# Mixer part of a hybrid decoder block: operands of the convolution half one block ahead, the output projection with that half first, loads and splits issued from inside the rows

## The chip, the cores and the metric

The kernel runs on one core of a Trainium2 chip. The metric is device microseconds (us) of one execution. The core has a matrix engine (PE, with its weight loads PEld), three elementwise engines (DVE, ACT, POOL) and a queue engine (SP) that issues DMA transfers; each engine takes its instructions strictly from its own list.

## The reference

One layer on a sequence of 2048 positions with 1024 channels, all in 32-bit floats:

```python
hn = rms_norm(x, g_pre_mix)
proj = hn @ w_in
y_ssm = s5_group_mixer(u_ssm, ...)      # ends in y * sigmoid(y @ w_glu)
y_conv = short_conv_mixer(h_conv, b_gate, c_gate, conv_w)
y = concatenate([rms_norm(y_ssm, g_ssm_out), rms_norm(y_conv, g_conv_out)], axis=-1)
x = x + rms_norm(y @ w_out, g_post_mix)
hn = rms_norm(x, g_pre_mlp)
m = square(relu(hn @ w_up)) @ w_down
x = x + rms_norm(m, g_post_mlp)
```

The change touches the lines from `sigmoid(y @ w_glu)` to `hn @ w_up`.

## The kernel before, in words

Every 32-bit product is made of three matmuls: each operand is split into a high and a low part (`split`, L167 to L169: ACT copies the high part, another engine subtracts it to get the low part), and `mm3` (L86 to L89) adds high by high, high by low and low by high.

The kernel runs in this order: input projections with the state-space part and the short convolution (results go to the DRAM tensors `y_d` and `yc_d`); then the mixer, which is what the change is about; then up (`product`, a scheme with seven products for eight) and down. The mixer works in four blocks of 512 positions:

- `yprep(blk)` (L688) loads four tiles of `y_d` and splits them; `glu(blk)` (L810) multiplies them by the gate weights, four groups of twelve matmuls in PSUM "B" (three buffers), takes the sigmoid on ACT, multiplies on DVE, scales and splits to `mh[blk]`, and adds up squares on POOL (`sumsq`, L788).
- `cprep(blk)` (L799) loads four tiles of `yc_d`, scales and splits them to `mc[blk]`, and adds up squares on DVE.
- `load_wo` (L834) loads and splits the sixteen 128x512 pieces of the output weights; `glu` takes two of its steps after each of its groups.
- `norms(blk, br)` (L847) sums the squares over the partitions with four small matmuls in PSUM "C" (one buffer), and DVE and POOL make the factor `rr` of it.
- `wout(blk)` (L868) makes four rows of 128 positions. A row is four groups of twelve matmuls in PSUM "A" (four buffers): two column halves with `mh` (br 0), then two with `mc` (br 1). ACT copies the first two to the row buffer `o` with the factor (L888), DVE adds the others (L892). Then comes a chain over the whole row: square on ACT, factor on POOL (`rstd`, L121, L122), DVE L898, square, factor, DVE L904; `x1_d` and `hn_d` are stored by SP (L899, L906).
- `hsum(0, t)` (L917) reads `hn_d` back (1 MB), makes five sums on DVE (L924) and stores them to `hs_d`; `xload` and `xbuild` (L929, L938) load a 1 MB operand of up and transpose it on PE; `wprep` (L1007) makes the weights of up.

The buffers that matter: `s2k` (nine of 2 KB a partition), `r4` (four rows, for `x`, for `o`, and for the raw `y` of odd blocks), `c8` (four) and `b8` (fourteen) of 8 KB. PE and POOL run the instructions in the order in which the code issues them; the lists of DVE, ACT and SP are put in order when the program is built. The blocks stand in this order: `cprep(0)`, `yprep(1)`, `glu(0)`, `glu(1)`, `yprep(2)`, `wout(0)`, `glu(2)`, `cprep(1)`, `yprep(3)`, `wout(1)`, `glu(3)`, `cprep(2)`, four `hsum`, `wout(2)`, `cprep(3)`, two `xload`, `wout(3)` with two `xbuild` in it, and then up with the first `wload`, two more `xload` and seven `wprep`.

## Time and profile before

| | us |
|---|---|
| median of 3 runs | 2021.76 |
| the runs | 2017.68 to 2022.14 |
| the profiled execution, its own time | 2021.03 |
| its span, first to last instruction | 2018.8 |
| PE busy in it | 1927.5 (95%) |
| DVE busy in it | 1423.1 (70%) |

The span is the time between the first and the last instruction; the profiled execution took 2.2 us more than its span. The busy time of PE is a modelled one: matmuls overlap, and each is shown with 0.39 us where a new one starts every 0.23 us. What PE lost is therefore read from its idle stretches, from what ended them, and from the granted clock.

### The profile page before, as it was taken

Reading aid. Unit: us, or ns where it says so; the run is one execution under the profiler, and the core shown is the slowest. Engines: PE = TensorE matmul, PEld = TensorE weight load, DVE = VectorE, ACT = ScalarE, POOL = GpSimd, SP = SyncE. Lnnn points to the kernel's source line nnn. Section 1 sums busy time; section 2 is a strip of 40 time slices with the busy share of each in tenths; the row PEclk is TensorE's granted clock in tenths of the full one; section 3 lists DMA queues with packets and bytes.
Section 4 is the critical chain, followed back from the end, with each engine's and each line's share of the span. In section 5 each row is a group of like instructions: output and inputs, shape, how many; then the busy total and the mean of one; then the engine's idle time right before and its main releaser. Section 6 shows DMA issues by size and latency. Waiting matters only on the chain.

```text
span 2018.8 us, 25420 instructions
## 1 busy us (share of the span) xinstructions
PE 1927.5 (95%) x8576; PEld 1573.8 (78%) x8576; DVE 1423.1 (70%) x2046; ACT 839.3 (42%) x1463; POOL 701.0 (35%) x704
## 2 busy tenths in 40 slices
PE   8789999997977989999999999999999999999997
PEld 6667877785755768888888888887888888888886
DVE  8748889858666669888878887876844444539564
ACT  6322232235433335555556555554433343235331
POOL 3295666404333223434432443441522102203220
PEclk9889999999988999999999999999999999999999
DMA  6432243125436655755447343426955545548634
GB/s 199 128 90 82 75 138 124 59 82 159 141 104 210 238 204 191 261 186 204 164 146 261 144 170 141 147 110 231 381 197 187 193 146 177 179 134 282 230 104 146
DMA packets 202002, 340.34 MB, mean 169 GB/s; under 512 B 56336, under 2 KB 64784, under 8 KB 199568
## 3 DMA queue, kind: packets, MB, share of 16 engines
q1 hardware_dynamic: 201728, 338.72, 49.4%
q8 instruction: 67, 1.10, 0.2%
q14 instruction: 63, 0.52, 0.1%
q10 hardware_dynamic: 144, 0.00, 0.0%
HBM read 230.51 MB, written 106.95 MB: 167 GB/s over the span
## 4 chain that ended last, share of the span: by engine, by line
PE 78%; DVE 6%; DMA 5%; issue 4%; POOL 4%; ACT 3%; SPq 0%; DVEq 0%; POOLq 0%; ACTq 0%
PE A L87 16%; PE A L89 16%; PE A L88 16%; PE mm L87 4%; PE B L87 4%; PE B L89 4%; PE B L88 4%; PE mm L88 4%; PE mm L89 4%; DMA raw<-in_xt_dram 2%; DMA s2k<-yc_d 1%; PE C L87 1%; PE C L89 1%; PE C L88 1%; PE B L947 1%
## 5 line engine op out<-in xcount | busy, mean ns | idle before, releaser
L1013 POOL TENSOR_TENSOR t<-b 128x512 f32<-128x512 f32 x155 | 247.0, 1616 | 364.0 <-DVE t L1047 109.3
L87 PE MATMUL A<-b,w 128*128 128x512 f32 x640 | 249.8, 390 | 0.0
L89 PE MATMUL A<-b,w 128*128 128x512 f32 x640 | 249.1, 389 | 0.0
L88 PE MATMUL A<-b,w 128*128 128x512 f32 x640 | 249.0, 389 | 0.0
L1093 POOL TENSOR_TENSOR t<-t,t 128x512 f32<-128x512 f32 x80 | 118.8, 1491 | 362.5 <-DMA t<-in_w_down_dram 358.1
L87 PE MATMUL mm<-xh,wh 128*128 128x512 f32 x496 | 200.4, 404 | 7.3 <-ACT wh L168 7.3
L88 PE MATMUL mm<-xl,wh 128*128 128x512 f32 x496 | 196.5, 396 | 2.6 <-DVE xl L152 2.6
L89 PE MATMUL mm<-xh,wl 128*128 128x512 f32 x496 | 196.0, 395 | 0.2 <-POOL wl L169 0.2
L169 DVE TENSOR_TENSOR b<-w,b 128x512 fp32r<-128x512 f32 x112 | 92.8, 869 | 131.3 <-ACT b L168 131.3
L87 PE MATMUL A<-b,c 128*128 128x512 f32 x448 | 175.1, 391 | 1.5 <-ACT b L168 1.5
L88 PE MATMUL A<-b,c 128*128 128x512 f32 x448 | 175.1, 391 | 0.6 <-DVE b L169 0.6
L89 PE MATMUL A<-b,c 128*128 128x512 f32 x448 | 174.8, 390 | 0.0
L1066 DVE TENSOR_TENSOR t<-t,t 128x512 f32<-128x512 f32 x160 | 127.8, 864 | 36.8 <-ACT t L1020 36.8
L169 DVE TENSOR_TENSOR w<-t,w 128x512 fp32r<-128x512 f32 x160 | 127.8, 814 | 35.8 <-ACT w L168 34.5
L169 DVE TENSOR_TENSOR c<-w,c 128x512 fp32r<-128x512 f32 x112 | 83.3, 782 | 96.1 <-ACT c L168 96.0
L89 PEld LDWEIGHTS A<-b,w 128*128 128x128 f32 x640 | 120.1, 188 | 25.0
L87 PEld LDWEIGHTS A<-b,w 128*128 128x128 f32 x640 | 120.1, 188 | 24.8
L88 PEld LDWEIGHTS A<-b,w 128*128 128x128 f32 x640 | 120.2, 188 | 24.5
L168 ACT ACTIVATE b<-w 128x512 fp32r<-128x512 f32 x112 | 64.6, 622 | 159.4 <-PE C L89 146.3
L87 PE MATMUL B<-b,b 128*128 128x512 f32 x336 | 130.7, 389 | 0.0
L88 PE MATMUL B<-b,b 128*128 128x512 f32 x336 | 130.7, 389 | 0.0
L89 PE MATMUL B<-b,b 128*128 128x512 f32 x336 | 130.7, 389 | 0.0
(421 smaller groups left out, 4439.5 us busy)
## 6 DMA issues: line engine op xcount, KB each, us to landing
hid_d<-t SPq DMA_DIRECT2D x224, 256.0 KB
w<-hid_d SPq DMA_DIRECT2D x224, 256.0 KB
t<-in_w_down_dram SPq DMA_DIRECT2D x192, 256.0 KB
b<-in_w_up_dram SPq DMA_DIRECT2D x64, 512.0 KB
raw<-in_xt_dram SPq DMA_DIRECT2D x48, 256.0 KB
raw<-in_w_cv_dram SPq DMA_DIRECT2D x48, 256.0 KB
b<-hs_d SPq DMA_DIRECT2D x10, 1024.0 KB
r<-in_x_dram SPq DMA_DIRECT2D x16, 512.0 KB
```

The costliest lines, as they stand in the source:

```text
L87: T.matmul(ps, lh, rh, start=start, stop=False)
L88: T.matmul(ps, lh, rl, start=False, stop=False)
L89: T.matmul(ps, ll, rh, start=False, stop=stop)
L168: A.activation(dst_h, raw, AF.Copy)
L169: eng.tensor_tensor(dst_l, raw, dst_h.bitcast(F32), op=ALU.subtract)
L947: T.transpose(pt[:, t * P:(t + 1) * P], r[:, t, k * P:(k + 1) * P], ident)
L1013: eng.tensor_tensor(src, q[0], q[1], op=pm_op[LEFT[j][1]])
L1066: V.tensor_tensor(src, q[0], q[1], op=pm_op[LEFT[j][1]])
L1093: G.tensor_tensor(r[0], r[0], r[1], op=pm_op[RIGHT[j][1]])
```

## The change

What was issued between the blocks is issued inside them. `yprep`, `cprep` and `hsum` become generators that first issue all their loads; `wout` takes a step of such a generator after each of its sixteen groups. `cprep(blk + 1)` runs within `wout(blk)`, and a row takes the `mc` half (br 1) first. The conv half of the output weights is loaded and split first, with the low parts on DVE as before; the low parts of the other half are made on POOL. The squares for the norms are made in place. `r4` is now two pools of two, `xx` and `o`. A new pool of eight 2 KB tiles (`w2a`) lives through mixer and up in place of `h2` and of half of the pool `w2` of up (the other half is `w2b`). `c8` now also holds `mc` of odd blocks. The first `wload`, three `xload`, four `wprep` and the two `xbuild` stand in `wout(3)`.

```diff
@@ def yprep @@
-        if blk % 2 == 1:
+        if blk == 1:
             a, b = c8(), c8()
...
+            rs = [t[:, 512 * j:512 * j + 512] for t in (r4("o"), r4("o")) for j in range(2)]
         else:
-            hl = [(h2(), h2()) for q in range(4)]
...
+            hl = [(w2a(), w2a()) for q in range(4)]
             rs = [s2k() for _ in range(4)]
...
+        yhl[blk] = hl
+        yield
+        for q in range(4):
...
             A.activation(nat(h), r, AF.Copy)
             V.tensor_tensor(nat(l), r, nat(h.bitcast(F32)), op=ALU.subtract)
+            yield
@@ def sumsq, def cprep @@
-    def sumsq(blk, br, i, src):
-        t = s2k()
+    def sumsq(blk, br, i, t):
         if br:
-            A.activation(t, src, AF.Square)
+            A.activation(t, t, AF.Square)
         else:
-            G.tensor_tensor(t, src, src, op=ALU.mult)
+            G.tensor_tensor(t, t, t, op=ALU.mult)
...
-        h, l = b8(), b8()
+        h, l = (c8(), c8()) if blk % 2 else (b8(), b8())
...
+        for i in range(-2, 4):
+            if i < 2:
+                raw[i + 2] = s2k()
+                nc.sync.dma_start(out=raw[i + 2], in_=yc_d[i + 2][:, blk * BLK:(blk + 1) * BLK])
+                if i < 0:
+                    continue
+            if i == 0:
+                yield
+            yc = raw[i]
@@ def glu, def load_wo @@
-            if blk and m == (3 if blk == 1 else 1):
-                norms(blk - 1, 0)
...
-        for h in range(2):
+        for h in (1, 0):
...
-                           w_out[k * P:(k + 1) * P, dh * 512:dh * 512 + 512], V)
+                           w_out[k * P:(k + 1) * P, dh * 512:dh * 512 + 512], V if h else G)
@@ def wout @@
-            for br, m in ((0, mh[blk]), (1, mc[blk])):
+            for br, m in ((1, mc[blk]), (0, mh[blk])):
...
-                    if t == 0 and dh == 0 and br == 1:
-                        norms(blk, 1)
-                        if blk == 2:
-                            norms(3, 0)
+                    if t == 0 and dh == 0:
+                        norms(blk, br)
                     rr = rrs[blk, br]
-                    if br == 0:
+                    if br:
                         A.activation(o[:, sl], ps, AF.Copy, scale=rr[:, t:t + 1])
...
+                    next(aside, None)
+            if t == 3:
+                run(aside)
@@ the order of the blocks @@
+    def first():
+        wload(0)
+        for j in ORDER[:2]:
+            xload(0, j)
+        yield
+        for i, j in enumerate(ORDER[:2]):
+            for n in ORDER[2 * i:2 * i + 2]:
+                yield
+                wprep(0, n, V, s2k)
+            yield from xbuild(0, j)
+        xload(0, ORDER[2])
+
+    wout(0, chain(yprep(2), cprep(1)))
+    glu(2)
+    wout(1, chain(yprep(3), cprep(2)))
+    glu(3)
+    wout(2, chain(cprep(3), *(hsum(0, t, lambda: c8(F32)) for t in range(4))))
+    wout(3, first())
@@ def wprep, def dload @@
-        h, l = w2(), w2()
+        h, l = (w2a(), w2a()) if j in ORDER[:4] else (w2b(), w2b())
...
-                raws = [[w2(F32)] for _ in range(2)]
+                raws = [[(w2b if side else w2a)(F32)] for _ in range(2)]
```

In the built programs SP issues 1225 transfers before and after, DVE has eight instructions fewer and POOL eight more. Three places show what moved.

The first is POOL at the end of `glu(1)`. These are its rows before (L793 and L797 are the squares and sums of the `glu` blocks, L860 is the factor of the first norms):

```order
L793 TENSOR_TENSOR s2k<-s2k 128x512 x2
L797 TENSOR_TENSOR s2k<-s2k 128x512
L793 TENSOR_TENSOR s2k<-s2k 128x512
L797 TENSOR_TENSOR s2k<-s2k 128x512
L793 TENSOR_TENSOR s2k<-s2k 128x512
L797 TENSOR_TENSOR s2k<-s2k 128x512
L860 TENSOR_TENSOR rr_4959<-sr,nhalf 128x4
```

And these are the rows there of the changed kernel, where the same three operations stand on L798, L802 and L871, and L170 is the low part of a piece of the output weights:

```order
L170 TENSOR_TENSOR b_4859<-s2k,b_4859 128x512
L170 TENSOR_TENSOR b_4860<-s2k,b_4860 128x512
L798 TENSOR_TENSOR s2k<-s2k 128x512
L802 TENSOR_TENSOR s2k<-s2k 128x512
L170 TENSOR_TENSOR b_4857<-s2k,b_4857 128x512
L170 TENSOR_TENSOR b_4858<-s2k,b_4858 128x512
L798 TENSOR_TENSOR s2k<-s2k 128x512
L802 TENSOR_TENSOR s2k<-s2k 128x512
L170 TENSOR_TENSOR b_4859<-s2k,b_4859 128x512
L170 TENSOR_TENSOR b_4860<-s2k,b_4860 128x512
L871 TENSOR_TENSOR rr_4974<-sr,nhalf 128x4
```

Two low parts stand behind each square of `glu(1)`, and the factor of the first norms stands behind the last of them.

The second place is SP, where the conv operands of block 1 are loaded. Before, the loads stand behind the stores of the last row of `wout(0)` (`x_d_93` and `hn_d_109`):

```order
L700 DMA r_5433<-y_d_85 128x8x64
L899 DMA x_d_93<-r_5232 128x1024
L906 DMA hn_d_109<-r_5234 256x1x512
L872 DMA r_5446<-in_x_dram 128x1024
L804 DMA s2k<-yc_d_86 128x512
L804 DMA s2k<-yc_d_87 128x512
L804 DMA s2k<-yc_d_88 128x512
L804 DMA s2k<-yc_d_89 128x512
```

In the changed kernel they stand ahead of the stores of the first row of `wout(0)`:

```order
L704 DMA s2k<-y_d_84 128x8x64
L704 DMA s2k<-y_d_85 128x8x64
L811 DMA s2k<-yc_d_86 128x512
L811 DMA s2k<-yc_d_87 128x512
L811 DMA s2k<-yc_d_88 128x512
L811 DMA s2k<-yc_d_89 128x512
L910 DMA x_d_90<-xx 128x1024
L917 DMA hn_d_106<-o 256x1x512
```

The loads moved from the end of the block to its first row, some three rows of `wout` earlier.

The third place is SP at the end of `wout(2)`. Before, the two operands of up (`b_6283`, `b_6285`, from `hs_d`) are loaded ahead of the stores of the block's last row (`x_d_101`, `hn_d_113`):

```order
L899 DMA x_d_100<-r_6104 128x1024
L906 DMA hn_d_112<-r_6106 256x1x512
L872 DMA r_6287<-in_x_dram 128x1024
L932 DMA b_6283<-hs_d_114 128x2048
L932 DMA b_6285<-hs_d_116 128x2048
L899 DMA x_d_101<-r_6179 128x1024
L906 DMA hn_d_113<-r_6181 256x1x512
```

In the changed kernel the stores of the last `hsum` (L937), those stores and the weights of up come first:

```order
L910 DMA x_d_100<-xx 128x1024
L917 DMA hn_d_112<-o 256x1x512
L937 DMA hs_d_114<-c_6108 128x512
L937 DMA hs_d_115<-c_6108 128x512
L937 DMA hs_d_116<-c_6108 128x512
L937 DMA hs_d_117<-c_6108 128x512
L937 DMA hs_d_118<-c_6107 128x512
L884 DMA xx<-in_x_dram 128x1024
L910 DMA x_d_101<-xx 128x1024
L917 DMA hn_d_113<-o 256x1x512
L986 DMA b_6282<-in_w_up_dram 128x1024 x2
L944 DMA b_6285<-hs_d_114 128x2048
```

The load of the first operand (`b_6285`) moved behind the stores of the last row; its first transposes on PE moved by one group only, from ahead of the last group of the first row of `wout(3)` to behind it.

## Rows read from the trace of the kernel before

**Rows 1.** Stages: window, its length, busy PE, PEld, DVE, ACT, POOL (instructions), clock, DMA share, GB/s.
```profile
455.80:511.50 55.70, 42.97 (x162) 31.48 (x162) 45.02 (x51) 29.63 (x47) 23.38 (x16) 0.88 0.56 164
511.50:556.10 44.60, 44.60 (x202) 36.98 (x201) 29.99 (x32) 20.93 (x31) 13.80 (x17) 1.00 0.39 130
556.10:616.70 60.60, 48.82 (x201) 38.04 (x200) 36.38 (x39) 18.36 (x31) 20.27 (x21) 0.92 0.30 102
616.70:628.50 11.80, 11.80 (x57) 9.88 (x56) 7.57 (x9) 5.26 (x9) 4.37 (x5) 1.00 0.28 100
628.50:694.70 66.20, 54.20 (x209) 42.20 (x209) 46.71 (x61) 23.65 (x40) 19.98 (x22) 0.82 0.75 254
694.70:747.10 52.40, 50.06 (x233) 41.33 (x231) 32.75 (x41) 18.86 (x33) 10.98 (x17) 0.97 0.58 206
747.10:763.00 15.90, 5.73 (x14) 3.93 (x14) 13.58 (x15) 6.23 (x11) 7.62 (x7) 0.61 0.91 327
770.00:1370.00 600.00, 600.00 (x2732) 499.10 (x2731) 498.20 (x675) 333.62 (x592) 238.53 (x150) 1.00 0.48 173
```

**Rows 2.** Waits of PE from 455 to 765: us in total, times, longest.
```profile
PE A L87 <- ACT b L805: 16.1, 4, 8.2
PE A L87 <- ACT w L168: 9.2, 1, 9.2
PE B L87 <- ACT s2k L819: 6.7, 4, 1.9
PE A L89 <- DVE b L806: 3.9, 4, 2.0
PE A L88 <- DVE b L169: 3.7, 4, 1.9
PE A L87 <- ACT r L888: 3.4, 2, 2.0
```

**Rows 3.** Timeline of PE around the second half of the first row of `wout(1)`.
```profile
558.53 0.39 PE L89 MATMUL A<-b,b 128*128 128x512 f32 x1
...
561.25 0.39 PE L89 MATMUL A<-b,b 128*128 128x512 f32 x1
569.80 0.79 PE L87 MATMUL A<-b,b 128*128 128x512 f32 x1 [8.17 <-ACT b L805]
...
572.24 0.63 PE L88 MATMUL A<-b,b 128*128 128x512 f32 x1
```

**Rows 4.** Groups of POOL from 455.8 to 511.5: busy us, mean ns, idle before.
```profile
L793 POOL TENSOR_TENSOR s2k<-s2k 128x512 f32<-128x512 f32 x8 | 10.9, 1367 | 32.2 <-DVE s2k L820 32.2
L797 POOL TENSOR_TENSOR s2k<-s2k 128x512 f32<-128x512 f32 x6 | 9.6, 1605 | 0.5
L860 POOL TENSOR_TENSOR rr<-sr,nhalf 128x4 f32<-128x4 f32 x2 | 2.9, 1428 | 2.7 <-DVE sr L857 2.7
```

**Rows 5.** Low parts (L169) on POOL and DVE: ns min/median/max, first and last start.
```profile
L169 DVE TENSOR_TENSOR b<-s2k,b x16: 676/686/1780, 475.6 to 509.0; 128x512 fp32r<-128x512 f32 x16
...
L169 POOL TENSOR_TENSOR wl<-raw,wh x4: 1322/1626/1831, 7.3 to 20.7; 128x512 fp32r<-128x512 f32 x4
```

**Rows 6.** Timeline of DVE: the chain of the last row of `wout(3)`.
```profile
746.75 0.75 DVE L892 SCALAR_TENSOR_TENSOR r<-A,rr,r 128x512 f32<-128x512 f32 x1 [1.44 <-PE A L89]
...
754.24 0.75 DVE L904 TENSOR_SCALAR r<-r,s 128x1024 f32<-128x1024 f32 x1 [0.92 <-POOL s L122]
```

**Rows 7.** Sums of `hsum` on DVE, 628 to 706: busy us, mean ns, idle.
```profile
L924 DVE TENSOR_TENSOR c<-c 128x512 f32<-128x512 f32 x20 | 13.5, 735 | 0.0
```

**Rows 8.** The critical chain: start, us; the load of an operand of up.
```profile
695.86 5.95 DMA b<-hs_d
```

**Rows 9.** Waits of the queue SP, 555 to 765: total us, times, longest.
```profile
SPq L920 <- DMA hs_d<-c: 3.3, 2, 3.2
```

**Rows 10.** DMA issues by line: count and KB of each.
```profile
hs_d<-c SPq DMA_DIRECT2D x20, 256.0 KB
...
c<-hn_d SPq DMA_DIRECT2D x4, 1024.0 KB
```

More of the change, by code (lines that the diff above doesn't have):

```diff
@@ L2 @@
 from contextlib import ExitStack
+from itertools import chain
 import concourse.bass as bass
@@ L656, in open_left @@
         pool("xl", "XL")
+        pool("sbw", "W")
         mid("sbl", "L")
@@ L667, in b8, with w2a, r4 @@
         return sb["XR"].tile([P, 4, 512], dt, name="b8", bufs=14)
-    def h2(dt=F32R):
-        return sb["L"].tile([P, 512], dt, name="h2", bufs=8)
+    def w2a(dt=F32R):
+        return sb["W"].tile([P, 512], dt, name="w2a", bufs=8)
     def s2k():
         return sb["L"].tile([P, 512], F32, name="s2k", bufs=9)
-    def r4():
-        return sb["R"].tile([P, D], F32, name="r4", bufs=4)
+    def r4(name):
+        return sb["R"].tile([P, D], F32, name=name, bufs=2)
     def small(name, n, bufs=2):
@@ L742, in block_kernel @@
                 open_left()
-                yprep(0)
+                run(yprep(0))
                 gluh, glul = c8(), c8()
@@ L799, in cprep @@
     def cprep(blk):
-        h, l = b8(), b8()
+        h, l = (c8(), c8()) if blk % 2 else (b8(), b8())
         mc[blk] = (h, l)
-        for i in range(4):
-            yc = s2k()
-            nc.sync.dma_start(out=yc, in_=yc_d[i][:, blk * BLK:(blk + 1) * BLK])
+        raw = {}
+        for i in range(-2, 4):
[7 more added lines that the diff above has]
+            yc = raw[i]
             A.activation(h[:, i, :], yc, AF.Copy, scale=gcv[:, i:i + 1])
@@ L826, in glu @@
             sumsq(blk, 0, m, sg)
[L827 to L828 removed]
             for _ in range(2):
                 next(wo_steps, None)
[L832 removed]
+    wo = {}
     def load_wo():
[L835 removed]
+        for h in (1, 0):
             for k in range(4 * h, 4 * h + 4):
[L837 removed]
+                wo[k] = b8()
             for dh in range(2):
@@ L866, in junk, with wout @@
         return sb["R"].tile([P, D], BF16, name="junk", bufs=1)
-    def wout(blk):
+    def wout(blk, aside=()):
+        aside = iter(aside)
         for t in range(4):
             tt = 4 * blk + t
-            xx = r4()
+            xx = r4("xx")
             nc.sync.dma_start(out=xx, in_=x[tt * P:(tt + 1) * P, :])
-            o = r4()
-            for br, m in ((0, mh[blk]), (1, mc[blk])):
+            o = r4("o")
+            for br, m in ((1, mc[blk]), (0, mh[blk])):
                 for dh in range(2):
@@ L940, in xbuild @@
         r = rows.pop((hf, j))
-        get = c8 if j in ORDER[:2] else b8
+        get = c8 if j in ORDER[:4:2] else b8
         h, l = get(), get()
@@ L950, in xbuild @@
             yield
-    steps = iter(())
-    def step(n=1):
-        for _ in range(n):
-            next(steps, None)
-    cprep(0)
+    run(yprep(1))
+    cprep0 = cprep(0)
+    next(cprep0)
     gss = sb["XR"].tile([P, 24], F32, name="gss", bufs=1)[:, :4]
     nc.sync.dma_start(out=gss, in_=g_ssm)
-    yprep(1)
+    run(cprep0)
     gpo = sb["R"].tile([P, D], F32, name="gp", bufs=1)
@@ L968, in block_kernel @@
     glu(1)
-    for _ in wo_steps:
-        pass
-    yprep(2)
-    wout(0)
-    glu(2)
-    cprep(1)
-    yprep(3)
-    wout(1)
-    glu(3)
-    cprep(2)
-    for t in range(4):
-        hsum(0, t, lambda: c8(F32))
-    wout(2)
-    cprep(3)
-    for j in ORDER[:2]:
-        xload(0, j)
-    steps = (None for j in ORDER[:2] for _ in xbuild(0, j))
-    wout(3)
-    pm_.close()
-    mid("sbu", "U")
-    def w2(dt=F32R):
-        return sb["U"].tile([P, 512], dt, name="w2", bufs=16)
-    def t2(shape=(P, 512), dt=F32):
-        return sb["U"].tile(list(shape), dt, name="t2", bufs=14)
+    run(wo_steps)
     NF = DFF // 256
@@ L1005, in wload, with wprep @@
             nc.sync.dma_start(out=r[:, 2 * i:2 * i + 2, :], in_=w_up[2 * f + i])
-    def wprep(n, j, eng=G):
+    def wprep(n, j, eng=G, tmp=None):
         r = wraw[n]
@@ L1011, in wprep, with w2b, t2 @@
         if len(q) > 1:
-            src = t2()
+            src = (tmp or t2)()
             eng.tensor_tensor(src, q[0], q[1], op=pm_op[LEFT[j][1]])
-        h, l = w2(), w2()
+        h, l = (w2a(), w2a()) if j in ORDER[:4] else (w2b(), w2b())
         split(h, l, src, V)
         W[n, j] = h, l
+    def first():
+        wload(0)
+        for j in ORDER[:2]:
+            xload(0, j)
+        yield
+        for i, j in enumerate(ORDER[:2]):
+            for n in ORDER[2 * i:2 * i + 2]:
+                yield
+                wprep(0, n, V, s2k)
[7 more added lines that the diff above has]
+    wout(3, first())
+    pm_.close()
+    mid("sbu", "U")
+    def w2b(dt=F32R):
+        return sb["U"].tile([P, 512], dt, name="w2b", bufs=8)
+    def t2(shape=(P, 512), dt=F32):
+        return sb["U"].tile(list(shape), dt, name="t2", bufs=14)
     def square(c):
@@ L1096, in dload @@
         opnd[j, s] = out_
-    wload(0)
-    xload(0, ORDER[2])
     xload(0, ORDER[3])
-    for j in ORDER:
+    for j in ORDER[4:]:
         wprep(0, j, V)
@@ L1127, in block_kernel @@
             if n in (2, 4, 6, 8):
-                hsum(1, n // 2 - 1, lambda: b8(F32))
+                run(hsum(1, n // 2 - 1, lambda: b8(F32)))
     gpl = [t2() for _ in range(2)]
```

16 lines of the change are left out of this document (5 added, 11 removed).

## The prediction, made before the result was known

> **What bounds the kernel now.** I read the stages first, then what PE waited for, then the timelines of those places. In the 600 us of up PE is busy all the time at full clock [rows 1]; the mixer is where it waits. What a stage would need without waits comes from two rows: twelve matmuls start within 561.25 - 558.53 = 2.72 us, so a group is 2.72 us [rows 3]; and the stretch 511.5 to 556.1, with PE busy throughout, holds sixteen groups and one set of norm matmuls, 44.6 = 43.5 + 1.1 [rows 1]. A block of `wout` with two sets of norms then needs 45.7 us, a `glu` 10.9. Against that the windows show [rows 1]: 455.8 to 511.5 (both first `glu`, first row, two norms) 55.7 where 12 groups and norms need 34.8, lost 20.9; `wout(1)` 60.6 against 44.6, lost 16.0; `wout(2)` 66.2 against 45.7, lost 20.5; `wout(3)` 52.4 against 47.2 (one set of norms, and eight sets of transposes, for which I take 0.32 each), lost 5.2; and 15.9 up to the end of the first product of up, which needs 2.7, lost 13.2. Together 76 us.
>
> The waits say why [rows 2]. 20.0 us are PE waiting for the conv operands (L805 on ACT, L806 on DVE): 8.2 in `wout(1)` and the rest in `wout(2)`. 9.2 us are the first weights of up. 10.4 us are the sigmoid of `glu` (L819) and the low parts of the output weights (L169), all before 511.5. 3.4 us are copies into row buffers (L888), in `wout(1)`, where the raw `y` of block 3 holds two of the four `r4`. The rest of the 76 is the clock: after the wait that ends at 569.80 a matmul shows 0.63 us instead of 0.39 [rows 3], and the granted clock is 0.82 in the stage of `wout(2)` and 0.61 at the start of up, against 1.00 where PE was kept busy [rows 1]; 1.00 is the upper of the two levels (2.4 GHz).
>
> **The change part by part.** The sum is made against the profiled execution, 2021.0 us, which is 0.7 below the median of the three runs.
>
> *First stage, to the second row of `wout(0)`: +6.* DVE gives eight low parts away, POOL takes them. On DVE they are 0.69 us by the median and up to 1.78 beside other work; on POOL 1.63 by the only four that it makes [rows 5], together 13.0 us. POOL has 23.4 us of work here and waits 35 [rows 4]. But the factor of the first norms, which before came behind fourteen squares and sums, now comes behind the eight low parts too, and the copy of the first PSUM buffer needs it; PE needs that buffer for the second row. If all low parts fit into POOL's idle time, the second row starts no later, and with the 3.7 us of waits for L169 gone up to 3 us earlier. If none does, it starts 13.0 later, less some 4 that PE waited at that place anyway: +9. They can't begin before the first square of `glu(1)`, and only half of the squares' idle time lies behind that, so I take +6, nearer to the upper end. The conv half going first costs nothing, its operands being ready long before.
>
> The Trainium skill ("GPSIMD Engine Reference", section Key points) says that POOL shares its SBUF interfaces with DVE, and that DVE is about twice as fast for elementwise work, which speaks against handing it the low parts. By that factor a low part would take 1.4 us there, eight 11.0, and the term would be +4; the row's 1.63 decides.
>
> *Rest of `wout(0)` and `glu(2)`: -1.* A set of norms leaves. `yprep(2)` and `cprep(1)` ride here: DVE was busy 30.0 of 44.6 and ACT 20.9 [rows 1]; the sixteen operations of `cprep(1)` and `yprep(2)` fit in.
>
> *`wout(1)`: -11.9.* Its conv operands are split a block earlier, so the 8.2 us wait and the slow clock behind it go, and with two `o` and two `xx` in every block also the 3.4 us. What is late next is the factor: on POOL the squares and sums of the `glu` ahead (four at 1.37, three at 1.61, 10.3 us [rows 4]) stand before it, and they start when DVE, still in the chain of the last row (8.2 us from its last L892 to the end of L904 [rows 6]), gets to `glu`. About 7 us for the first group and its split (an estimate: 2.7, and four operations of about 1), 8.2 of chain, 10.3 and 1.4 make 27; PE wants the buffer 10.9 + 10.9 + 2.2 = 24 us after `glu` began. So 3 us of waiting (0 if the chain is through in time, 6 if DVE lags): 48.7 instead of 60.6. `glu(3)` loses the set of norms in it, -0.9.
>
> *`wout(2)`: -17.5.* The same, 48.7 instead of 66.2. But the four `hsum` are now in this block, and with two of the four `c8` holding `mc[3]` they have one pair: the next load waits until the last store has landed. One turn is a 1 MB load of 5.95 us [rows 8], five sums of 0.735 [rows 7] and the landing of the stores, 3.2 us of waiting seen [rows 9]: 12.8, four turns 51 us from some 6 us after the block begins. That is longer than the block; the last sums come about 6 us after its last matmul, in DVE's list ahead of the last row's chain.
>
> *`wout(3)`: +7.4.* In SP's list the first operand of up now comes behind the store of that last row and 1 MB of weights. Row chain 8.2 and some 5 of late sums put that store 13 us after the block's end; weights and operand, 2 MB, take the 5.95 us in which before two operands were loaded together [rows 8], and issue time: landed at 20 to 22. PE reaches the transposes after the first row, 10.9 + 2.2 = 13 us. The wait is some 9 us, and I add 2.5 for the lower clock behind it: twelve matmuls at 0.63 instead of 0.39 [rows 3] are 2.9. So 47.2 + 1.1 + 9 + 2.5 = 59.8 instead of 52.4. Bounds: 3 us of waiting if the last sums are in time, 25 if a turn takes 17 us.
>
> The Trainium skill ("DMA: Bandwidth & Descriptors", section Specifications) gives about 358 GB/s of HBM for a core. No stage here shows more than 327 GB/s, at a DMA share of 0.91 [rows 1]. With 20 stores of 256 KB and four 1 MB loads [rows 10] and twelve 512 KB row transfers `wout(2)` moves 16.8 MB: 51 us at the row's rate, 47 by the page. Either is longer than the 45.7 that PE needs.
>
> *Start of up: -13.2.* Two operands and four weights are there, so the first product takes 2.7 us. The other three weights and two operands come product by product, as before.
>
> *Free edits.* Squares in place wait for the split that reads the same tile, on engines that have slack there (POOL busy 20 of 66 us, ACT 24 [rows 1]); they spare an `s2k` each. In up a weight's buffer is now free one product later, 2.7 us; it is made six products ahead, and that cover hides it. Without it the cost would be up to 2.7 us a product.
>
> Sum: +6 - 1 - 11.9 - 0.9 - 17.5 + 7.4 - 13.2 = -31.1: 2021.0 - 31.1 = **1990 us**.
>
> **The rivals.**
> *The new waits are hidden:* POOL keeps up (-3), factors are in time (0), and the operand lands 3 us late with no loss of clock: 9 + 6 + 8.5 better, 1967. For it: POOL idles 35 us in the first stage. Against it: the order on SP and the 51 us of `hsum`.
> *The queues eat most of it:* +9 in the first stage, 6 us at each factor, 25 us for the operand: 3 + 6 + 16 worse, 2015. For it: DVE is busy 46.7 us in the stage of `wout(2)` now [rows 1], nearly all of the 48.7 that it is to take, and its list stands still behind every late load.
> *Slower, through up:* the four weights in `w2a` have four pairs for four products, so ACT's copy for the next round must wait for the product that it follows, and in ACT's list that wait can hold up the copies of PSUM. There are 32 rounds; at 1 us each the whole 31 is gone, at 1.5 it is 2038. Against it: PE has no idle time in up now, ACT is busy 334 of 600 us, though DVE is at 498 [rows 1].
> *The loads come late all the same:* nine `s2k` must hold four raw `y`, four `yc` and up to three sums, so SP could wait at the conv loads as now. They need only be there a block later, so this gives back at most the 20.0 us of these waits and their clock: no change. The sums of block 0 are read in its first row, and free their tiles then.
>
> A measurement of this kernel can tell a change from none at about 0.2%, 4 us.
>
> **How the numbers follow.** The forecast, 20 to 45 us faster (1976 to 2001), 0.52; hidden waits, below 1976, 0.20; queues, 4 to 20 us faster, 0.17; no change 0.04; slower 0.07. So faster 0.89, same 0.04, slower 0.07. The range goes from 1966, the hidden case, to 2012, near the queue case; some 0.2 lie outside.
>
> **What the changed profile would show.** Right: no wait of PE for the conv operands (now L817, L818), none of 9 us before the first product of up, and `wout(1)` and `wout(2)` each below 50 us; POOL's low parts at about 1.6 us, its first factor after 515; one wait of some 9 us at the transposes of `wout(3)`, ended by a DMA. The prediction is wrong if PE waits inside up, if `hsum` takes more than 17 us a turn, or if DVE falls so far behind in `wout(2)` that PE waits for its PSUM buffers.

## The result and the profile after

The changed kernel takes 1999.39 us (median of four runs, 1997.44 to 2000.01), the kernel before 2021.95 (2017.68 to 2027.06) beside it: a ratio of 0.9887, with a 95% interval of 0.9875 to 0.9900. It is faster by 1.1%, within the forecast of 1976 to 2001 and the range of 1966 to 2012, and 9.4 us above the sum of 1990. The profiled execution took 1999.82 us with a span of 1998.0; before it was 2018.8, so the spans differ by 20.8 us.

The first view after is again the windows, laid on the same pieces of the program as [rows 1] and on two at the start of up (columns: window, its length, busy PE, PEld, DVE, ACT, POOL with the number of instructions, granted clock, DMA share, GB/s):

```profile
456.98:513.57 56.59, 42.46 (x160) 30.74 (x160) 37.30 (x40) 28.00 (x46) 32.52 (x24) 0.85 0.56 167
513.57:558.86 45.29, 45.29 (x193) 37.35 (x194) 34.82 (x39) 24.43 (x40) 13.18 (x18) 0.96 0.35 129
558.86:606.60 47.74, 46.62 (x210) 37.48 (x209) 35.07 (x39) 23.20 (x36) 19.32 (x21) 1.00 0.44 139
606.60:617.48 10.88, 10.88 (x50) 9.01 (x49) 8.19 (x10) 4.50 (x8) 3.52 (x5) 1.00 0.39 145
617.48:667.66 50.18, 46.66 (x209) 37.33 (x208) 37.59 (x49) 17.64 (x30) 19.01 (x19) 1.00 0.68 226
667.66:733.00 65.34, 54.10 (x240) 44.42 (x241) 40.25 (x53) 22.60 (x39) 12.31 (x20) 0.90 0.67 226
733.00:735.89 2.89, 2.89 (x15) 2.37 (x14) 1.34 (x2) 1.15 (x2) 0.54 (x1) 1.00 0.68 103
735.89:768.10 32.21, 28.06 (x152) 22.88 (x151) 29.79 (x42) 22.12 (x41) 11.40 (x10) 0.95 0.74 285
770.00:1370.00 600.00, 600.00 (x2706) 498.41 (x2705) 497.92 (x669) 340.12 (x585) 237.37 (x150) 1.00 0.49 177
```

`wout(1)` and `wout(2)` (third and fifth row) run at full clock and have lost most of their waits: 0.9 us is left in the one, 3.1 in the other. `wout(3)` (sixth) has become the longest block, and the first eight products of up (the two rows ahead of the last) are not free of waits either; the 600 us of up are as before. Laid beside the trace before, stage by stage and in us, with the ends of the stages taken from the first matmul of the next (that of `wout(3)` before, behind which PE stood, from its last transposes):

| stage | before | after | difference | forecast |
|---|---|---|---|---|
| second row of `wout(0)` begins at | 511.35 | 513.57 | +2.2 | +6 |
| rest of `wout(0)`, `glu(2)` | 44.7 | 45.3 | +0.6 | -1 |
| `wout(1)` | 60.7 | 47.7 | -13.0 | -11.9 |
| `glu(3)` | 11.8 | 10.9 | -1.0 | -0.9 |
| `wout(2)` | 66.1 | 50.2 | -15.9 | -17.5 |
| `wout(3)` | 52.4 | 65.3 | +12.9 | +7.4 |
| to the end of the first product of up | 16.0 | 2.9 | -13.1 | -13.2 |
| from there to the end of the span | 1255.6 | 1262.1 | +6.5 | 0 |
| sum | | | -20.8 | -31.1 |

Of the last difference 5.9 us lie in the first round of up: from the end of the first product to the start of the eighth it is 26.4 us before (763.17 to 789.57) and 32.3 after (735.89 to 768.15). In the nine runs below that leave this round's code as it is, it is 30.4 to 32.9. The waits of PE from 455 to 765, which answer to [rows 2] (engine, tile and line that waited, what ended it; us in total, times, longest; for the same code a line number here is one above that of before in the helpers, as L170 for L169, and ten to thirteen further down):

```profile
PE C L959 <- DMA b<-hs_d: 7.4, 2, 7.0
PE A L89 <- POOL b L170: 6.9, 6, 2.3
PE B L88 <- ACT s2k L832: 6.4, 3, 2.6
PE A L88 <- ACT o L898: 4.7, 4, 2.0
PE C L861 <- DVE sr L866: 4.2, 1, 4.2
PE C L959 <- DVE b L961: 2.9, 1, 2.9
```

The 20.0 us for conv operands and the 9.2 us for the first weights of up are gone. New are 6.9 us for low parts on POOL (L170) in place of 3.7 on DVE, 4.2 us at the second norms of `wout(3)` (L861) and 7.0 us at its first transposes (L959), where before PE waited 2.3 us in all, and 2.9 us in up. The timeline of PE shows the last two of `wout(3)`:

```profile
681.34 1.84 PE L861 MATMUL C<-ones,s2k 128*128 128x1 f32 x8 [4.22 <-DVE sr L866]
683.04 0.77 PE L88 MATMUL A<-b,b 128*128 128x512 f32 x1
683.61 0.63 PE L89 MATMUL A<-b,b 128*128 128x512 f32 x1
...
695.21 1.09 PE L959 MATMUL C<-ident,b 128*128 128x128 f32 x4 [7.02 <-DMA b<-hs_d]
695.95 0.78 PE L88 MATMUL A<-b,c 128*128 128x512 f32 x1
```

Behind the first wait a matmul shows 0.63 us, the mark of the lower clock that [rows 3] had in `wout(1)`: the group that starts at 683.04 takes 5.2 us from its first start to its last end, the one at 695.95 3.9, and the one at 674.23, ahead of the waits, 2.9.

What is late there is told by DVE (the sums of `hsum`, L936, and what the line that reads the norms waits behind) and by SP (loads of `hsum` L931, its stores L937, the store of a row L917, the weights L986, the operand L944):

```profile
649.68 1.29 DVE L936 TENSOR_TENSOR c<-c 128x512 f32<-128x512 f32 x2 [1.62 <-DMA c<-hn_d]
...
663.08 3.10 DVE L936 TENSOR_TENSOR c<-c 128x512 f32<-128x512 f32 x5 [2.53 <-DMA c<-hn_d]
...
676.88 3.10 DVE L936 TENSOR_TENSOR c<-c 128x512 f32<-128x512 f32 x5 [3.94 <-DMA c<-hn_d]
...
681.03 0.15 DVE L866 TENSOR_TENSOR sr<-C,rho 128x4 f32<-128x4 f32 x1
...
684.67 0.75 DVE L915 TENSOR_SCALAR o<-o,s 128x1024 f32<-128x1024 f32 x1 [0.78 <-POOL s L123]
```

```profile
627.17 1.26 SPq L931 DMA_DIRECT2D c<-hn_d  x1
...
643.76 0.32 SPq L931 DMA_DIRECT2D c<-hn_d  x1
...
656.38 0.32 SPq L931 DMA_DIRECT2D c<-hn_d  x1
...
669.97 0.32 SPq L931 DMA_DIRECT2D c<-hn_d  x1
...
677.60 2.75 SPq L937 DMA_DIRECT2D hs_d<-c  x5
...
685.46 0.52 SPq L917 DMA_DIRECT2D hn_d<-o  x1
686.07 1.30 SPq L986 DMA_DIRECT2D b<-in_w_up_dram  x2
687.46 0.92 SPq L944 DMA_DIRECT2D b<-hs_d  x2
```

The four loads of `hsum` follow one another in turns of 16.6, 12.6 and 13.6 us. The fourth sums begin at 676.88, after the block's end at 667.66, and DVE's read of the norms, the store of the last row, and the operand of up come behind them, one after the other.

### The profile page after: what moved, and what is told of

It is laid out like the page before. It is cut to its first block, busy times and chain, and to the rows that moved or that the text cites. A ratio compares the mean times of both kernels' runs of the same rounds, so it can differ in the third digit from the quotient of the medians.

```text
span 1998.0 us, 25431 instructions
## 1 busy us (share of the span) xinstructions
PE 1917.8 (96%) x8576; PEld 1567.3 (78%) x8576; DVE 1409.6 (71%) x2038; ACT 848.5 (42%) x1463; POOL 703.5 (35%) x712
## 4 chain that ended last, share of the span: by engine, by line
PE 61%; DMA 1%; DVE 1%; issue 1%; ACT 0%; POOL 0%; SPq 0%; DVEq 0%; POOLq 0%; ACTq 0%
PE A L89 15%; PE A L88 15%; PE A L90 15%; PE B L88 4%; PE B L90 4%; PE B L89 4%; PE C L88 1%; PE C L90 1%; PE C L89 1%; PE B L959 1%; DMA b<-hs_d 1%; PE C L959 0%; DMA t<-x_d 0%; DMA w2a<-hid_d 0%; DVE t L1216 0%
## 5 line engine op out<-in xcount | busy, mean ns | idle before, releaser
L1104 POOL TENSOR_TENSOR t<-t,t 128x512 f32<-128x512 f32 x80 | 111.0, 1393 | 363.1 <-DMA t<-in_w_down_dram 340.8
L88 PE MATMUL A<-b,c 128*128 128x512 f32 x512 | 201.5, 394 | 3.8 <-ACT o L898 2.9
L89 PE MATMUL A<-b,c 128*128 128x512 f32 x512 | 200.3, 391 | 1.0 <-DVE b L170 1.0
L90 PE MATMUL A<-b,c 128*128 128x512 f32 x512 | 200.2, 391 | 0.0
L170 DVE TENSOR_TENSOR b<-w2b,b 128x512 fp32r<-128x512 f32 x112 | 88.3, 827 | 135.2 <-ACT b L169 135.2
L170 DVE TENSOR_TENSOR c<-w2a,c 128x512 fp32r<-128x512 f32 x112 | 81.0, 762 | 98.5 <-ACT c L169 98.5
L88 PE MATMUL A<-b,w2b 128*128 128x512 f32 x384 | 150.4, 392 | 0.0
L89 PE MATMUL A<-b,w2b 128*128 128x512 f32 x384 | 149.9, 390 | 0.0
L90 PE MATMUL A<-b,w2b 128*128 128x512 f32 x384 | 149.8, 390 | 0.0
L169 ACT ACTIVATE b<-w2b 128x512 fp32r<-128x512 f32 x112 | 64.7, 623 | 159.1 <-PE C L90 145.7
L169 ACT ACTIVATE c<-w2a 128x512 fp32r<-128x512 f32 x112 | 64.9, 623 | 138.0 <-PE A L90 137.1
L88 PEld LDWEIGHTS mm<-xh,wh 128*128 128x128 f32 x496 | 94.5, 190 | 33.1 <-ACT wh L169 7.6
L88 PEld LDWEIGHTS A<-b,c 128*128 128x128 f32 x512 | 96.6, 189 | 25.2 <-ACT o L898 4.2
L89 PEld LDWEIGHTS A<-b,c 128*128 128x128 f32 x512 | 96.8, 189 | 21.3 <-DVE b L170 1.3
```

Source lines behind the costliest of these rows:

```text
L88: T.matmul(ps, lh, rh, start=start, stop=False)
L89: T.matmul(ps, lh, rl, start=False, stop=False)
L90: T.matmul(ps, ll, rh, start=False, stop=stop)
L169: A.activation(dst_h, raw, AF.Copy)
L170: eng.tensor_tensor(dst_l, raw, dst_h.bitcast(F32), op=ALU.subtract)
L1104: G.tensor_tensor(r[0], r[0], r[1], op=pm_op[RIGHT[j][1]])
```

## The experiments

All times are medians of four or more runs, and each ratio is to the kernel before, run beside it on the same chip; ratios are what is compared between runs (the changed kernel: 0.9887). "First stage" is the time from the first matmul of `glu(0)` to that of the second row of `wout(0)`: 54.7 us before, 56.6 in the changed kernel. It repeats well: the changed kernel and the four runs below that leave the order and the low parts of this stage alone show 56.6 to 56.7, and the four in which DVE makes all low parts and nothing else there differs show 52.5 to 53.1.

**The conv operands again at the end of the glu.**

```diff
-    wout(0, chain(yprep(2), cprep(1)))
+    wout(0, yprep(2))
     glu(2)
-    wout(1, chain(yprep(3), cprep(2)))
+    run(cprep(1))
+    wout(1, yprep(3))
     glu(3)
+    run(cprep(2))
```

> The conv operands of blocks 1 and 2 are again split at the end of the glu ahead of their block, as in the kernel before; all else is as in the changed kernel (1999.4 us). Theory (the gain of wout(1) and wout(2), 13.0 and 15.9 us, is that the conv operands are there a block early): PE waits for them again at the first conv matmuls of both blocks, 8 us or more each since no ssm groups stand ahead of them now, with the clock halved behind each; some 13 us in wout(1) and 13 in wout(2) come back, about 2025 us. Rival (the gain is from two o and two xx in every block and from sets of norms that left): conv waits of at most 2 us in each block, at most 2006 us.

Measured: 2013.97 us, ratio 0.9968 (0.9957 to 0.9979), 0.8% above the changed kernel. The waits are back (the list of waits of PE, as above):

```profile
PE A L88 <- ACT c L817: 7.1, 1, 7.1
PE A L88 <- ACT b L817: 7.1, 1, 7.1
```

From the end of the `glu` ahead, `wout(1)` takes 60.2 us and `wout(2)` 59.8, 12.5 and 9.7 more than in the changed kernel; `wout(3)` gets 5.4 shorter, and its wait at the norms is gone, as if a slower `wout(2)` left `hsum` more time. The theory holds for the waits and the two blocks, and the rival falls; the total is 11 us below the expected one. Nearly all of `wout(1)`'s gain of 13.0, and 9.7 of the 15.9 of `wout(2)`, come from having the conv operands a block early.

**The low parts on DVE again.**

```diff
-                           w_out[k * P:(k + 1) * P, dh * 512:dh * 512 + 512], V if h else G)
+                           w_out[k * P:(k + 1) * P, dh * 512:dh * 512 + 512], V)
```

> The low parts of the ssm half's output weights are made by DVE again, all else as in the changed kernel (1999.4 us). Theory (the eight low parts on POOL cost the first stage 2 us and more: the factor of the first norms comes behind them): the second row of wout(0) starts 2 to 6 us earlier than 513.6, 1994 to 1997 us. Rival (DVE is what sets the pace in this stage, and is relieved by POOL): the second row starts at 514 to 519 with waits for L169 on DVE, 2000 to 2005 us.

Measured: 1991.16 us, ratio 0.9856 (0.9839 to 0.9873). The first stage takes 52.6 us, 4.0 less than in the changed kernel, and the second row no longer starts at the lower clock. In place of six waits for POOL, 6.9 us in all, PE has one of 5.8 us at the second norms and three short ones for DVE's low parts:

```profile
PE C L861 <- DVE sr L866: 10.4, 2, 5.8
...
PE A L89 <- DVE b L170: 0.9, 3, 0.5
```

(5.8 of the first line are in this stage, the other 4.6 in `wout(3)`.) So POOL's low parts cost 4.0 us there, and some 2 more by the ratios behind it: the theory holds, and the rival falls.

**hsum ahead of the conv operands of block 3.**

```diff
-    wout(2, chain(cprep(3), *(hsum(0, t, lambda: c8(F32)) for t in range(4))))
+    wout(2, chain(*(hsum(0, t, lambda: c8(F32)) for t in range(4)), cprep(3)))
```

> In wout(2) the four hsum steps stand ahead of the split of the conv operands of block 3, so that they find two pairs of c8 free; all else as in the changed kernel (1999.4 us). Theory (one pair of c8 makes the turns of hsum follow one another at 13 us each, the fourth sums come after the block's end, and they make the 4.2 us wait at the second norms of wout(3), part of the 7.0 at its transposes, and the lower clock behind both): the four loads are issued within some 30 us, the fourth sums are done before the block's last matmul, the wait at the norms is gone and that at the transposes 4 us or less, 1989 to 1993 us. Rival (the DMA volume of the block, or the weights ahead of the operand on SP, set these waits): the loads are issued earlier but land no earlier, 1997 to 2000 us. Against both: the conv operands of block 3 may now be late at the start of wout(3), which would show as a wait for L817 or L818 there.

Measured: 1981.16 us, ratio 0.9809 (0.9792 to 0.9826), 0.8% below the changed kernel and about twice the gain expected. `wout(2)` and `wout(3)` in the windows view:

```profile
617.00:666.40 49.40, 47.45 (x210) 38.59 (x208) 40.56 (x52) 18.03 (x31) 19.99 (x21) 0.97 0.79 272
666.40:716.80 50.40, 49.57 (x240) 40.98 (x241) 35.57 (x47) 22.08 (x39) 13.38 (x20) 1.00 0.61 216
```

`wout(3)` falls from 65.3 to 50.4 at full clock. The loads of `hsum` are issued at 603.9, 621.1, 625.5 and 641.4, and its last sums hardly wait for their load:

```profile
647.38 3.10 DVE L936 TENSOR_TENSOR c<-c 128x512 f32<-128x512 f32 x5 [0.28 <-DMA c<-hn_d]
...
678.42 0.75 DVE L915 TENSOR_SCALAR o<-o,s 128x1024 f32<-128x1024 f32 x1 [0.44 <-POOL s L123]
```

The rival falls: the block moves its bytes in 49.4 us, at 272 GB/s where the changed kernel shows 226, so the volume did not set the turns. One thing more moved with the edit: the first operand of up now stands in SP's list ahead of the last row's store (issued at 670.9, the store at 679.2) and the weights ahead of both. So the 14.9 us are the price of late `hsum` with all that is queued behind it, not of one wait. The conv operands of block 3 came in time.

**The first weights of up after the last row again.**

```diff
     def first():

-        wload(0)
         for j in ORDER[:2]:
             xload(0, j)
         yield
         for i, j in enumerate(ORDER[:2]):
             for n in ORDER[2 * i:2 * i + 2]:
                 yield
-                wprep(0, n, V, s2k)
...
+    wload(0)
     xload(0, ORDER[3])
-    for j in ORDER[4:]:
+    for j in ORDER:
```

> The weights for the first four products of up are loaded and made after the last row again, as in the kernel before; the operands of the first two products are still made during the last rows. All else as in the changed kernel (1999.4 us). Theory (the 13.1 us at the start of up come from having the weights there): the operand lands some 3 us earlier in wout(3), but PE waits 6 to 9 us for the first weights at the start of up, with the lower clock behind it; about 2005 to 2008 us. Rival (what counts is the operand's early build; the seven pairs of DVE's sums and splits only move, and the 5.7 us lost in up's first round go with them): within 3 us of 1999.4.

Measured: 2008.62 us, ratio 0.9941 (0.9925 to 0.9957); its profile, from the fastest of its six runs, has a span of 2002.5. Two rows of the waits:

```profile
PE A L88 <- ACT w2a L169: 11.7, 1, 11.7
...
PE C L959 <- DMA b<-hs_d: 3.9, 1, 3.9
```

The first product ends 17.0 us later after the end of `wout(3)`, but `wout(3)` is 3.4 shorter, for the operand has no 1 MB of weights ahead of it and the wait is 3.9 instead of 7.0; and from the end of the first product to the start of the eighth it takes 25.1 us instead of 32.3. So of 17.0 us some 10 are given back around it. The theory holds, with a longer wait for the weights than it had. The early weights are worth their place, 0.5% by the ratios, but less than the 13 us that the stage at the start of up shows.

**Both good edits at once.**

```diff
-                           w_out[k * P:(k + 1) * P, dh * 512:dh * 512 + 512], V if h else G)
+                           w_out[k * P:(k + 1) * P, dh * 512:dh * 512 + 512], V)
...
-    wout(2, chain(cprep(3), *(hsum(0, t, lambda: c8(F32)) for t in range(4))))
+    wout(2, chain(*(hsum(0, t, lambda: c8(F32)) for t in range(4)), cprep(3)))
```

> Both edits at once: DVE makes the low parts of the ssm half's output weights, and in wout(2) the hsum steps stand ahead of the split of block 3's conv operands. Alone the first came out at 1991.2 us and the second at 1981.2, where the changed kernel has 1999.4. Theory (two costs at different places, the one before 514 us, the other after 670): they add, 1973 us, 1971 to 1976. Rival (what is gained early is waited for later, since DVE and the queues of wout(2) are then the pace): 1978 to 1982 us.

Measured: 1974.47 us, ratio 0.9770 (0.9755 to 0.9785), 1.17 percentage points below the changed kernel's, where the two alone gave 0.31 and 0.78: they add, as the theory has it. This is the fastest kernel of the study, 2.3% faster than the one before. First stage, `wout(2)` and `wout(3)`:

```profile
456.18:508.70 52.52, 42.01 (x160) 33.00 (x161) 45.55 (x49) 30.45 (x48) 23.41 (x16) 0.87 0.61 182
611.00:660.50 49.50, 47.59 (x209) 38.37 (x207) 40.75 (x53) 17.97 (x31) 19.98 (x21) 0.97 0.78 271
660.50:710.20 49.70, 49.65 (x241) 41.01 (x242) 35.40 (x47) 22.03 (x40) 14.19 (x20) 1.00 0.60 219
```

**Its last weights of up deferred.** On that kernel, the three pairs for the last products of up's first round come one after each operand build.

```diff
-    for j in ORDER[4:]:
-        wprep(0, j, V)
...
                     if len(builds) > 1:
                         xload(*builds[1])
+                if n == 0 and at < 3:
+                    wprep(0, ORDER[4 + at], V)
```

> As the kernel with both edits, and besides the first round's last three pairs of up's weights are made one after each of the first three operand builds, not all three ahead of them. Theory (in the first round of up the copies out of PSUM of the operands stand on DVE behind three pairs of weights, and this is what makes the round longer than before): the waits of PE on DVE for L961 in the first 30 us of up go, 1 to 3 us faster than the kernel with both edits, 1970 to 1972 us. Rival (the loads of the operands from DRAM set the round): the waits move to the loads, within 1 us of it.

Measured: 1980.31 us, ratio 0.9800 (0.9786 to 0.9815): 0.3% slower than the kernel with both edits. The theory falls: the first round takes 35.8 us instead of 30.7, and PE's wait for DVE at L961 grows from 2.2 to 5.8. DVE has no wait of more than 0.7 us from 714 to 745 in the kernel with both edits, and with the weights deferred it has this one ahead of them:

```profile
DVE t L1045 <- DMA hn_d<-o: 3.4, 1, 3.4
```

(The line takes the second product out of PSUM. PE had ended that product at 718.9, and what DVE waits for is a DMA that lands at 726.4, put down to the store of the last row. The line writes to a new tile, which may lie where the row buffer lay; this is not shown.) The early place had filled that idle time; deferred, the weights stand in a busier one.

**The ssm half first.** On the kernel with all low parts on DVE.

```diff
-        for h in (1, 0):
+        for h in (0, 1):
...
-            for br, m in ((1, mc[blk]), (0, mh[blk])):
+            for br, m in ((0, mh[blk]), (1, mc[blk])):
...
-                    if br:
+                    if not br:
```

> DVE makes all low parts of the output weights, and the ssm half goes first again in every row and in the making of the weights, as in the kernel before; the rest as in the changed kernel. It is to be read against the run with low parts on DVE and the conv half first (1991.2 us). Theory (the conv half first is worth something in the first stage alone, where glu(1) and the low parts go on while it runs): the second row of wout(0) starts 2 to 5 us later than 508.4, with waits for L170 or the sigmoid of the glu; 1993 to 1997 us. Rival (the order of the halves costs and gains nothing, as the forecast had it): the second row at 507 to 509.5, 1990 to 1992 us.

Measured: 1994.71 us, ratio 0.9876 (0.9859 to 0.9892), against 0.9856 (0.9839 to 0.9873); the spans are 1989.5 and 1989.1. The first stage takes 53.0 us, 0.4 more and within the spread: the rival, that the order of the halves is worth nothing there, holds for this stage. Behind it `wout(1)` is 1.7 us longer and `wout(2)` 2.1, and `wout(3)` 2.4 shorter. The median lies where the theory had it, but by total time the two can't be told apart.

**Half of the low parts on POOL.** On the kernel with both edits.

```diff
-                           w_out[k * P:(k + 1) * P, dh * 512:dh * 512 + 512], V)
+                           w_out[k * P:(k + 1) * P, dh * 512:dh * 512 + 512], V if h or k % 2 else G)
```

> As the kernel with both edits, but every second low part of the ssm half is made by POOL, four on POOL and four on DVE. Theory (with all eight on POOL the factor of the first norms comes late, with all eight on DVE DVE is late for the sums of the second norms, a wait of 5.8 us; POOL has idle time for four at 1.4 us): the wait at the norms falls to some 3 us and none comes at the weights, 2 to 3 us faster than the kernel with both edits, about 1970 us. Rival (POOL's squares set the first factor, and anything put between them is late): 1 to 4 us slower than it, 1974 to 1977 us.

Measured: 1980.77 us, ratio 0.9800 (0.9785 to 0.9814), 0.3% slower than the kernel with both edits. The wait of 5.8 us at the norms is gone, and PE waits for POOL instead:

```profile
PE A L89 <- POOL b L170: 6.0, 3, 3.5
```

The theory falls. The rival holds in sign, with 6 us where it had 1 to 4. But only 1.3 us of it lie in the first stage (53.9 against 52.5); 1.8 more are in `wout(1)`, 1.0 in `wout(2)` and 1.6 in the first round of up, and no run shows why.

**The conv operands of block 0 first.** On the kernel with all low parts on DVE.

```diff
-    run(yprep(1))
-    cprep0 = cprep(0)
-    next(cprep0)
+    run(cprep(0))
     gss = sb["XR"].tile([P, 24], F32, name="gss", bufs=1)[:, :4]
     nc.sync.dma_start(out=gss, in_=g_ssm)
-    run(cprep0)
+    run(yprep(1))
```

> DVE makes all low parts, and the conv operands of block 0 are loaded and split ahead of the raw y of block 1, as in the kernel before, not behind it; to be read against the run with low parts on DVE alone (1991.2 us, second row of wout(0) at 508.4). Theory (the first stage lost less than forecast since DVE no longer stands for the loads of block 0's conv operands, which end while it splits the y of block 1; before, its L806 waited 3.7 us there): 2 to 4 us of DVE's waiting come back at L818, the second row comes 2 to 4 us later, 1993 to 1996 us. Rival (that wait lay beside others and was worth nothing): second row within 1 us of 508.4, 1990 to 1992 us.

Measured: 1990.90 us, ratio 0.9864 (0.9849 to 0.9879): no difference. The first stage takes 53.4 us against 52.6, little beyond the spread, and DVE does not stand at L818; the rival holds.

**The second norms in another PSUM buffer.** On the changed kernel.

```diff
-        pq = pst("C", (P, 4))
+        pq = pst("C" if br else "B", (P, 4))
```

> As the changed kernel (1999.4 us), but the sums of the second norms go to one of the three PSUM buffers B, not to the one buffer C, so PE needn't wait for DVE to read the first set. Theory (the 4.2 us wait at the norms of wout(3) and the 7.0 us at its transposes stand in a row before the same late work: the operand lands at 695.1 whatever PE does before): the first wait goes and the second grows by as much; wout(3) within 1.5 us of 65.3, 1997 to 2000 us. Rival (the one buffer C costs the 4.2 us by itself): wout(3) some 4 to 6 us shorter, with the lower clock behind the first wait gone too, 1993 to 1995 us.

Measured: 1998.07 us, ratio 0.9892 (0.9876 to 0.9909): the same. The wait at the norms is gone, and the one at the transposes has taken its place:

```profile
PE C L959 <- DMA b<-hs_d: 16.2, 2, 14.8
```

Its longest is 14.8 us and ends at 695.7, where it ended at 695.2 before; `wout(3)` takes 67.1 us, slightly more than the theory allowed, and the rival's gain does not come. The theory holds: the two waits are one.

**POOL makes the last weights of up's first round.** On the kernel with both edits.

```diff
-    def wprep(n, j, eng=G, tmp=None):
+    def wprep(n, j, eng=G, tmp=None, low=V):
...
-        split(h, l, src, V)
+        split(h, l, src, low)
...
-        wprep(0, j, V)
+        wprep(0, j, G, low=G)
```

> As the kernel with low parts on DVE and hsum first (1974.5 us), but POOL makes the sums and low parts of the last three pairs of up's first weights, which DVE made. Theory (DVE has no idle time in the first 27 us of up and is what makes its first round longer than before): five operations, some 6 us, leave its list; the waits of PE on DVE for L961 there (0.5 and 2.2 us) and the lower clock go, 2 to 4 us faster, 1970 to 1972 us. Rival (the loads of the operands set the round, and DVE's copies come late because of them): waits move to the loads or to POOL's weights, 1973 to 1977 us.

Measured: 1980.31 us, ratio 0.9812 (0.9797 to 0.9826), 0.4% slower than the kernel with both edits. The theory falls: the first round takes 35.4 us instead of 30.7, and the wait at L961 is 4.5 us. DVE's waits from 714 to 745, in the same form as those of PE:

```profile
DVE b L961 <- ACT b L960: 3.1, 1, 3.1
DVE w2b L170 <- ACT w2b L169: 2.0, 1, 2.0
DVE w2a L170 <- ACT w2a L169: 1.8, 1, 1.8
```

Freed of five operations, DVE idles 3.1 us for an operand that is not built yet, and later 3.8 for weights; the sums of the next round's weights, ahead of these in POOL's list before, come behind the new work there (POOL's ten sums and low parts run from 721.7 on).

**The ssm half's squares not in place.** On the kernel with all low parts on DVE.

```diff
-    def sumsq(blk, br, i, t):
+    def sumsq(blk, br, i, src):
+        t = src if br else s2k()
...
-            G.tensor_tensor(t, t, t, op=ALU.mult)
+            G.tensor_tensor(t, src, src, op=ALU.mult)
```

> DVE makes all low parts, and POOL's squares of the ssm half go to a second s2k buffer again and not in place, as in the kernel before (the conv half's stay in place); to be read against the run with low parts on DVE alone (1991.2 us, second row of wout(0) at 508.4). Theory (sparing an s2k for each square is what made the first stage 3 us shorter beside the cost of POOL's low parts: the sigmoid and the weight loads find a free s2k earlier): second row at 510.5 to 512.5, with longer waits at the sigmoid of glu; 1993 to 1996 us. Rival (the forecast's: the squares in place are worth nothing, the buffers being free in time): second row within 1 us of 508.4, 1990 to 1992 us.

Measured: 1993.41 us, ratio 0.9865 (0.9848 to 0.9881). The first stage takes 54.3 us, 1.7 more, about what it took before the change; the longest wait for the sigmoid goes from 2.7 to 3.2 us, and those for DVE's low parts from 0.9 to 4.4 in all. By the stage the squares in place are worth some 1.7 us (1.2 to 1.8 against the four runs without this edit), less than the theory's 3 and more than the rival's nothing; by total time it is not resolved.

## Why the prediction was right, and where it was off

The sum missed by 10.3 us: 5.5 in `wout(3)`, 6.5 in up, 1.6 each in `wout(2)` and the rest of `wout(0)`, less 3.8 in the first stage and 1.1 in `wout(1)`. The terms err by 15.2 us one way and by 4.9 the other, so that the total is no further off is in part luck.

*The main gain* was as forecast, in place and size. `wout(1)` gave 13.0 (11.9 forecast), `wout(2)` 15.9 (17.5), the start of up 13.1 (13.2). No wait for conv operands is left, and undoing that one part brought 12.5 and 9.7 us of it back. The factor, for which 3 us were taken in each block, was in time in `wout(1)`, whose one wait of 0.9 us is for a later copy into `o`. In `wout(2)` it cost 1.1 us, as DVE and PE show, and 1.95 more are waited at the end for a copy into `o`:

```profile
630.58 0.16 DVE L873 TENSOR_TENSOR rr<-rr,rho 128x4 f32<-128x4 f32 x1 [2.17 <-POOL rr L871]
631.57 0.50 PE L88 MATMUL A<-b,b 128*128 128x512 f32 x1 [1.15 <-ACT o L898]
```

The volume of the transfers, which was to fill more than PE's 45.7 us, did not set the block. The items named come to 15.7 MB (16.8 with the four loads of conv operands), but 226 GB/s over 50.2 us are 11.3 MB: the rest fell outside the block, the fourth turn of `hsum` behind its end. With `hsum` first the block moved 272 GB/s in no more time, and 327 GB/s is no ceiling: the kernel before moves 381 from 1415 to 1465.

*The first stage*: the term of +6 was +2.2 (+1.9 from the first matmul of `glu(0)` on). Its mechanism was right: PE waits for low parts on POOL, and the first factor starts behind the last of them, at 511.5. It was mis-sized by two things. The low parts cost 4.0, shown by moving them back. By groups of POOL in 456.98 to 513.57 (busy us, mean ns, idle before) a part took 1.47 us where [rows 5] gave 1.63, and the factor (L871) 1.02 where [rows 4] gave 1.43:

```profile
L170 POOL TENSOR_TENSOR b<-s2k,b 128x512 fp32r<-128x512 f32 x8 | 11.6, 1466 | 0.0
...
L871 POOL TENSOR_TENSOR rr<-sr,nhalf 128x4 f32<-128x4 f32 x2 | 2.0, 1018 | 0.3 <-DVE sr L870 0.3
```

DVE, relieved of the low parts, stood idle while POOL made the last four of them:

```profile
512.58 0.16 DVE L873 TENSOR_TENSOR rr<-rr,rho 128x4 f32<-128x4 f32 x1 [9.38 <-POOL rr L871]
```

The estimate from the Trainium skill ("GPSIMD Engine Reference", Key points: DVE about twice as fast for elementwise work), 11.0 us and +4, was nearer than the one from the row: the trace has 11.6 us, and the low parts cost 4.0. That is in part luck, for in this stage the two engines do not differ by a factor of two: a part took 1.47 us on POOL and, in the run that moved them back, 1.21 on DVE.

The other thing is the squares in place, forecast at nothing and worth about 1.7; 4.0 less 1.7 is what was measured. The order of the halves and the place of block 0's conv operands, both tried, made 0.4 and 0.8, where runs of one code differ by up to 0.6.

*`wout(3)`*: the step that failed in size is "the last sums come about 6 us after its last matmul", and with it +7.4. The turn of 12.8 was right (16.6, 12.6, 13.6), but the first load was issued 9.7 us into the block, not 6, the first turn was 16.6, and the fourth sums ended 14.3 us after the last matmul at 665.7. Counted from that matmul, the row's store came at 19.7 instead of 13, and the operand landed at 29.4 instead of 20 to 22. That the same lateness would show first at the second norms, where DVE's one read of PSUM "C" stands behind the fourth sums in its list, was not foreseen; the run with the other buffer shows that it is the same wait and costs nothing more. The weights ahead of the operand are some 3 us of it. `hsum` issued first takes 14.9 us off the block, which is more than the whole error.

*Start of up and "free edits"*: -13.2 at the start was right, but the cover of that stall was forgotten. Before, the chain of the last row [rows 6] and the making of the first weights ran while PE stood. Now PE goes on at once, and the chain, the copies of the operands and the weights meet in its first round: DVE is busy 31.1 of the 35.1 us from 733.00 to 768.10, PE waits for it, and 5.9 us of the gain are given back. By the prediction's own sign it is wrong here, since PE waits inside up. That this round is short when PE stands ahead of it was seen with the weights late (25.1 us against 32.3); no run shows more of the cause. What in it would have to go first is open: deferring three pairs of weights and giving them to POOL both made it longer. The remaining 0.6 us of up is less than what the part behind the eighth product differs by from run to run (1227.2 to 1231.7).

*The other signs*: POOL's first factor was to come after 515 and came at 511.5; `wout(2)` was to stay below 50 us and took 50.2; the other signs came as named, with the wait of some 9 us at the transposes split into 4.2 and 7.0.

*The rivals*: the hidden waits came for the factor of `wout(1)` alone. Of "the queues eat most of it" the first-stage part did not come; its operand part did, in small: `wout(3)` took 5.5 us more than forecast, not 16. "Slower, through up" did not show: from 770 on PE is busy 600.00 of 600 us, as in [rows 1]. "Loads late all the same" did not come.

## What to carry to other kernels

When a stall is removed, list what ran in its shadow: that work does not go away, and here the next stage took back 5.9 of 13 us. Give the scarce buffers of a ring to the chain whose result is awaited last: with one pair of buffers the four turns of `hsum` were in series, and putting them ahead of the other user of these buffers, one line, gave 0.8% where the whole change gave 1.1%. Two waits in a row on different engines can be one late event; move the first away before you count both.

## What the runs showed of the hardware

The granted clock fell and came back within one block: with 4.2 us of idle PE the matmuls behind it run at 0.63 us instead of 0.39 for 4 us, and after the 7.0 us of idling that follow they do so for 2 us; over the block the granted clock is 0.90. With `hsum` first, without these two waits, it stayed at 1.00.

POOL and DVE can take longer for the same operation when both work at once. These are two pairs of low parts on POOL in the changed kernel, the first with DVE at work from 499.00 on, the second while DVE stood:

```profile
498.30 3.21 POOL L170 TENSOR_TENSOR b<-s2k,b 128x512 fp32r<-128x512 f32 x2
...
504.27 2.49 POOL L170 TENSOR_TENSOR b<-s2k,b 128x512 fp32r<-128x512 f32 x2
```

Before, ten of DVE's sixteen took 0.68 to 0.69 us, and six took 1.54 to 1.78, each of the six with a POOL operation beside it for 1.2 us or more, and none of the ten for more than 0.52. The mean was 1.07, and 1.21 in the run that moved eight low parts back. What makes them longer, no run here tests.
